# Weight sums by accumulating transfers, parts of 4, 6, 6 and 6, and square sums behind the chain in a two-layer decoder trunk

## The chip, the cores and the metric

The kernel runs on one core of one Trainium2 chip. The metric is the device time of one execution in microseconds (us). It was timed in three runs before the change: median 2678.73 us, from 2677.65 to 2682.8. The times inside an execution come from one profiled execution. Engines are named as the profile names them: PE (matmul), PEld (its weight load), DVE (vector), ACT (scalar), POOL (GpSimd), SP (sync). SP issues most transfers, POOL the others; L12 is line 12 of the kernel before.

## The reference

Two layers, each with an FFN, a mixer (retention and a short gated convolution in parallel) and a second FFN, all with RMS norms before and after, over 512 prompt tokens and 32 sample tokens. All in float32. What the change touches is the FFN and the norms between the phases:

```
def rmsnorm(x, g):
    xf = x.astype(jnp.float32)
    y = xf * lax.rsqrt(jnp.mean(xf * xf, axis=-1, keepdims=True) + NORM_EPS)
    return (y * g.astype(jnp.float32)).astype(x.dtype)

def swiglu(x, w_up, w_down):
    gate, up = jnp.split(x @ w_up, 2, axis=-1)
    return (jax.nn.silu(gate) * up) @ w_down

def layer(x, pos, s0, buf0, norms, w_ffn1_up, w_ffn1_down, w_in, conv_w, w_ret_out, w_conv_out, w_o,
          w_ffn2_up, w_ffn2_down):
    h = x + 0.5 * rmsnorm(swiglu(rmsnorm(x, norms[0]), w_ffn1_up, w_ffn1_down), norms[1])
    m, s_new, buf_new = mixer(rmsnorm(h, norms[2]), pos, s0, buf0, w_in, conv_w, w_ret_out, w_conv_out, w_o)
    h = h + rmsnorm(m, norms[3])
    h = h + 0.5 * rmsnorm(swiglu(rmsnorm(h, norms[4]), w_ffn2_up, w_ffn2_down), norms[5])
    return h, s_new, buf_new
```

The model width is 1024, the FFN width 2816; the mixer's input projection has 64 tiles of 128 columns.

## The kernel before, in words

Tokens lie on the free axis: 544 in two halves of 272. Features lie on the 128 partitions, so the width of 1024 is 8 tiles. A float32 product is made of three matmuls of a reduced format: both operands are cut into a rounded part and a rest (hi and lo for weights, xh and xl for data), and hi·xh, hi·xl and lo·xh are summed in PSUM. Cutting a weight tile is one ACT copy (whi) and one DVE subtraction (wlo).

There are six phases: FFN, mixer, FFN, then the same for the second layer. A phase is a list of jobs, run in order on PE. A plain `Job` (`run`, L335) makes one output tile of 128 features: 8 steps over the width, two halves, three matmuls, 48 in all. A `Pair` (`run_pair`, L353) makes two such tiles (gate and up, of one FFN tile) by seven products in place of eight, 7 × 12 = 84 matmuls in place of 96. The seven products read four weight sets: A (the first weight tile w1 as it is), and with w1 = [a1 a2] and w2 = [b1 b2] the sums s1 = a1 + b1, s3 = b1 + b2 (set 13), s2 = s3 + a1, s4 = s2 + a2 (set 24), and b2 itself (set 22). On the data side they read sums of x that are built once for a phase by `build_ops` (ops b, oh, ol; L587 to L600 and L264). The products run in the order A, 13, 24, A, 13, 24, 22 (the third one, with set 24, adds into a bank that ACT seeds at L194 from the first product's bank).

`PARTS` (L31) cuts the 22 tiles of the FFN width into four parts. In the first, gate and up are plain jobs (`PLAIN_PARTS`), in the others pairs. Behind a part's gate and up jobs come its 8 down jobs, whose length goes with the part's width: n tiles wide is n × 6 matmuls. So the FFN has 17 pairs (a mixer has 17 as well), 102 in all. `BUILD_AT` (L33) names the jobs of the FFN behind which the four `build_ops` are called.

Weights come by SP from HBM into `raw` tiles (L229), `RAW_BUFS` = 3 of them in turn; cut weights live in `w` tiles, `W_BUFS` = 14. A pair's preparation is a list of steps (`pair_steps`, L267): `s_a` cuts A; `s_13` adds s1 and s3 on DVE (L278, L279), `s_24` adds s2 and s4 on DVE (L284, L285) and frees w1's raw tile, which issues the next load; `c_24`, `c_13` and `c_22` cut the sets, the last frees w2's raw tile. `run_pair` calls one step behind each product, for the pair that follows, and `run` calls up to two steps of pairs up to `LOOK` = 4 jobs ahead. From such program order the tile framework makes each engine's queue and its semaphores; code under `urgent` (the seed L194, the evacuations) is moved ahead in it.

At the five boundaries between phases (`boundary`) the order on DVE, ACT and POOL is written out by hand as a script of events with times. The last `TAIL` = 5 down jobs of the old phase and the first `HEAD` = 5 jobs of the new one are run half by half, so that the norm of one half lies beside the matmuls of the other. For each half `chain` makes, for each of 8 tiles, a scaling (L1165), an add to the residual x (L1169), xh on ACT and xl (L1150), and the square (ACT L442) that DVE adds into acc (L444, the last one L448). Then `rstd` sums acc over features on PE (L469, a matmul with ones), and ACT L481 and DVE L482 to L484 make r, the factor of the norm, by which the evacuations multiply (L512, L520). `SUMS` holds the times of the square sums in the script, `RSTD_HEAD` that of the sum over features, `later_prep` cuts weights at given times.

Of the kernel before, what the change touches and what calls it, by code (L numbers as in the profile page):

```python
# [9 lines left out]
F32 = mybir.dt.float32  # L10
F32R = mybir.dt.float32r
AF = mybir.ActivationFunctionType  # L12
ALU = mybir.AluOpType
# [14 lines left out]
P = 128  # L28
KT = DM // P
FT = DFF // P  # L30
PARTS = [(0, 5), (5, 10), (10, 15), (15, 22)]  # L31
PLAIN_PARTS = 1
BUILD_AT = (6, 9, 11, 13)  # L33
CONV_PLAIN = 2
BUILD_MIX = (0, 2, 4, 5)
EPS = 1e-6
# [8 lines left out]

I_Q, I_K, I_V, I_G, I_BG, I_CG, I_XC, I_GR, I_GC = 0, 4, 8, 16, 24, 32, 40, 48, 56

RAW_BUFS = 3
W_BUFS = 14
LOOK = 4  # L50
U_BUFS = 54
T_BUFS = 14
# [7 lines left out]
LAST_B = 1.2  # L60
ONES_B = 4.2
CHAIN_B = 5.0
SUMS = 11.0, 19.0
URGENT = 300
RSTD_HEAD = 17.5, 22.5


def log_gammas():
# [63 lines left out]
class Trunk:  # L132
# [76 lines left out]
    def plan(self):  # L209

        for i, j in enumerate(self.jobs):
            if isinstance(j, Pair):
                a, b = self.to_load(j.w1), self.to_load(j.w2)
                self.steps += [(i, fn) for fn in self.pair_steps(i, a, b)]
            else:
                self.load_of[i] = a = self.to_load(j.w)
                self.steps.append((i, lambda i=i, a=a: self.prep_hi(i, a)(self.nc.vector)))
            self.last_step[i] = len(self.steps)
# [5 lines left out]
    def load(self, upto):  # L224
        while self.n_loaded < min(upto, len(self.loads)):
            w = self.loads[self.n_loaded]
            n = w.shape[1]
            r = self.wp.tile([P, 1024], F32, tag="raw", bufs=RAW_BUFS, name=self.name("raw"))
            self.nc.sync.dma_start(out=r[:, :n], in_=w)  # L229
            self.raw[self.n_loaded] = (r, n)  # L230
            self.n_loaded += 1

# [31 lines left out]
        self.nc.vector.tensor_tensor(out=lo, in0=r, in1=hi.bitcast(F32), op=ALU.subtract)  # L264
        return hl

    def pair_steps(self, i, a, b):  # L267
        nc, d = self.nc, {}
        hl = self.hl[i] = {}
        H = slice(0, 512), slice(512, 1024)  # L270

        def s_a():
            hl["A"] = self.cut(self.parts_of_weights(), self.loaded(a)[0])

        def s_13():
            ra, rb = self.loaded(a)[0], self.loaded(b)[0]
            s = d["13"] = self.w("s13", F32)
            nc.vector.tensor_tensor(out=s[:, H[0]], in0=ra[:, H[0]], in1=rb[:, H[0]], op=ALU.add)  # L278
            nc.vector.tensor_tensor(out=s[:, H[1]], in0=rb[:, H[0]], in1=rb[:, H[1]], op=ALU.add)  # L279

        def s_24():
            ra, s1 = self.raw[a][0], d["13"][:, H[1]]
            s = d["24"] = self.w("s24", F32)
            nc.vector.tensor_tensor(out=s[:, H[0]], in0=s1, in1=ra[:, H[0]], op=ALU.add)  # L284
            nc.vector.tensor_tensor(out=s[:, H[1]], in0=s[:, H[0]], in1=ra[:, H[1]], op=ALU.add)  # L285
            self.freed(a)

        def c_24():
            hl["24"] = self.cut(self.parts_of_weights(), d.pop("24"))

        def c_13():
            hl["13"] = self.cut(self.parts_of_weights(), d.pop("13"))

        def c_22():
            v = self.w("v")
            hl["22"] = self.cut((v[:, H[0]], v[:, H[1]]), self.raw[b][0][:, H[1]])
            self.freed(b)

        return [s_a, s_13, s_24, c_24, c_13, c_22]

    def step_on(self, n, upto=10 ** 6):
        while n > 0 and self.n_stepped < len(self.steps) and self.steps[self.n_stepped][0] < upto:
# [192 lines left out]
    def ffn_jobs(self, ph):  # L495
# [4 lines left out]
        ph["y"] = {}  # L500
        for pi, (p0, p1) in enumerate(PARTS):
            hh = {}
# [51 lines left out]
            def dn(m, pi=pi, p0=p0, p1=p1, hh=hh):  # L554
                last = pi == len(PARTS) - 1

# [600 lines left out]
    def chain(self, ev, at, ph, nxt, half):  # L1157

        nc, s = self.nc, self.hs(half)
        ts = {}  # L1160
        step = STEP if nxt else 0.8

        def scale(f):
            t = ts[f] = self.t("yg")
            nc.vector.tensor_tensor(out=t, in0=ph["y"][f][:, s], in1=ph["ry"][:, s], op=ALU.mult)  # L1165

        def add(f):
            x = self.x[f][:, s]
            nc.vector.tensor_tensor(out=x, in0=x, in1=ts.pop(f), op=ALU.add)  # L1169
            if nxt is None:  # L1170
                nc.sync.dma_start(out=self.a["y"][f, :, s], in_=x)

        for f in range(KT):
            t = at + step * f
            ev(t, lambda f=f: scale(f))
            ev(t + step + 0.4, lambda f=f: add(f))
            if nxt is not None:
                ev(t + step + 0.8, lambda f=f: self.pre_hi(nxt, f, half))
                ev(t + 2 * step + 0.8, lambda f=f: self.pre_lo(nxt, f, half))
                ev(SUMS[half] + 0.45 * f, lambda f=f: self.pre_sum(nxt, f, half, None, nc.vector))  # L1180

    def finish(self, ev, ph, d):

# [52 lines left out]
    def boundary(self, ph, nxt, i):  # L1236
# [3 lines left out]
        nc, script = self.nc, []  # L1240
# [7 lines left out]
        d = len(mvs[0]) * 3 * MM  # L1248
# [27 lines left out]
        if nxt is None:  # L1276
            self.finish(ev, ph, d)
        else:
            ev(LAST_B, lambda: ph["last"].pop()())
            ev(ONES_B, lambda: self.rstd([ph["yacc"][:, self.hs(1)]], 1, ph["ry"], DM))  # L1280
            self.chain(ev, CHAIN_B, ph, nxt, 1)
            V, G = nc.vector, nc.gpsimd
            self.head_script(ev, nxt, i + TAIL)
            for hi, lo in ((tb + d + 0.3, tb + d + 1.3), (tb + 2 * d + 0.3, tb + 2 * d + 1.3), (1.0, 2.0), (6.0, 7.0),
                           (14.0, 15.0)):
                self.later_prep(ev, hi, lo, V)
        self.play(script)
        if nxt is not None:
# [24 lines left out]
    def head_script(self, ev, nxt, i0):  # L1313

        nc = self.nc
        d = KT * 3 * MM
        if nxt["kind"] == "mix":
            self.mix_start(nxt)
        banks, out = [], []

        def copy(n, half):
            if half == 0:
                out.append(self.u("out"))
            nc.scalar.activation(out=out[n][:, self.hs(half)], in_=banks[half][n][:, :HALF], func=AF.Copy)  # L1324
            self.give(banks[half][n])

        for half in range(2):
            banks.append(self.head_part(ev, half * HEAD * d, nxt, i0, half))
            for n in range(HEAD):
                ev((HEAD * half + max(3, n + 1)) * d + 0.1 + 0.3 * n * (n < 3), lambda n=n, half=half: copy(n, half))  # L1330

        def rest(half):
            todo = []
            first = (3, 4) if nxt["kind"] == "mix" else ()
            for n in (*first, *(n for n in range(HEAD) if n not in first)):
                if n == 0 and first:
                    self.mix_tables(nxt, half)
                todo.append(self.jobs[i0 + n].evac(half, out[n][:, self.hs(half)]))
            for fn in todo:
                if fn:  # L1340
                    fn()

        for half in range(2):
            ev(RSTD_HEAD[half], lambda half=half: self.rstd([nxt["acc"][:, self.hs(half)]], half, nxt["r"], DM))
        ev(RSTD_HEAD[1] + 0.1, lambda: rest(0))
        nxt["rest"] = rest

    def head_side(self, nxt):
# [199 lines left out]
```

## Time and profile before

| what | value |
| --- | --- |
| median of three runs | 2678.73 us (2677.65 to 2682.8) |
| the profiled execution's own time | 2677.17 us |
| its span, first to last instruction | 2675.3 us |
| granted clock of PE | 0.997 of full speed |
| PE busy | 2628.3 us, 98%, 20718 matmuls recorded |
| DVE, ACT, POOL busy | 1861.0 (70%), 1354.0 (51%), 237.3 us (9%) |
| bytes moved by DMA | 296.86 MB, 111 GB/s over the span |

The profile counts the time of an engine in instructions as busy; matmuls are pipelined, so a busy PE need not be at its peak. The trace gives, for each instruction, when it started and what ended the idle time before it.

### The profile page before, as it was taken

Reading aid. Unit: us, or ns where it says so; the run is one execution under the profiler, and the core shown is the slowest. Engines: PE = TensorE matmul, PEld = TensorE weight load, DVE = VectorE, ACT = ScalarE, POOL = GpSimd, SP = SyncE. Lnnn points to the kernel's source line nnn. Section 1 sums busy time; section 2 is a strip of 40 time slices with the busy share of each in tenths; the row PEclk is TensorE's granted clock in tenths of the full one; section 3 lists DMA queues with packets and bytes.
Section 4 is the critical chain, followed back from the end, with each engine's and each line's share of the span. In section 5 each row is a group of like instructions: output and inputs, shape, how many; then the busy total and the mean of one; then the engine's idle time right before and its main releaser. Section 6 shows DMA issues by size and latency. Waiting matters only on the chain. (4 is left out here: it accounts for less than half of the span.)

```text
span 2675.3 us, 50606 instructions
## 1 busy us (share of the span) xinstructions
PE 2628.3 (98%) x20718; PEld 2606.1 (97%) x20718; DVE 1861.0 (70%) x3213; ACT 1354.0 (51%) x2546; POOL 237.3 (9%) x375
## 2 busy tenths in 40 slices
PE   9999999999999999999999999999999999999998
PEld 9999998999999999999999999999999999999997
DVE  6756748677986487667488557587678764875673
ACT  6555554434553455555555555544345434655553
POOL 1000021222100100000100000211210001000002
PEclk9999999999999999999999999999999999999999
DMA  4233344333343432332432334343333433323332
GB/s 155 83 96 102 105 142 148 116 107 120 103 132 104 133 106 83 99 103 86 130 118 84 101 95 144 114 147 105 111 116 101 130 104 121 118 83 95 102 105 90
DMA packets 91977, 296.86 MB, mean 111 GB/s; under 512 B 12064, under 2 KB 16288, under 8 KB 91744
## 3 DMA queue, kind: packets, MB, share of 16 engines
q1 hardware_dynamic: 74592, 235.46, 28.9%
q0 software_dynamic: 17152, 58.16, 6.3%
q8 instruction: 162, 2.65, 0.4%
q14 instruction: 71, 0.58, 0.1%
HBM read 266.17 MB, written 27.41 MB: 110 GB/s over the span
## 5 line engine op out<-in xcount | busy, mean ns | idle before, releaser
L324 PE MATMUL banks<-oh,whi 128*128 128x272 f32 x2040 | 588.6, 289 | 3.0 <-ACT banks L194 1.6
L324 PE MATMUL banks<-oh,wlo 128*128 128x272 f32 x2040 | 587.9, 288 | 0.0
L324 PE MATMUL banks<-ol,whi 128*128 128x272 f32 x2040 | 586.6, 288 | 0.0
L324 PE MATMUL banks<-xh,whi 128*128 128x272 f32 x1600 | 455.2, 298 | 9.6 <-ACT out L1324 8.7
L324 PE MATMUL banks<-xl,whi 128*128 128x272 f32 x1600 | 442.4, 289 | 0.0
L252 ACT ACTIVATE whi<-raw 128x1024 fp32r<-128x1024 f32 (+2 forms) x273 | 253.5, 931 | 313.3 <-PE banks L324 248.4
L256 DVE TENSOR_TENSOR wlo<-raw,whi 128x1024 fp32r<-128x1024 f32 (+2 forms) x273 | 291.2, 1068 | 150.5 <-ACT whi L252 117.6
L324 PEld LDWEIGHTS banks<-oh,whi 128*128 128x128 f32 x2040 | 383.8, 188 | 6.4 <-ACT banks L194 2.8
L324 PE MATMUL banks<-hh,whi 128*128 128x272 f32 x1408 | 385.2, 289 | 0.1
L324 PE MATMUL banks<-hl,whi 128*128 128x272 f32 x1408 | 384.5, 288 | 0.2
L324 PEld LDWEIGHTS banks<-ol,whi 128*128 128x128 f32 x2040 | 384.5, 188 | 0.0
L324 PEld LDWEIGHTS banks<-oh,wlo 128*128 128x128 f32 x2040 | 383.9, 188 | 0.0
L324 PE MATMUL banks<-xh,wlo 128*128 128x272 f32 x1600 | 371.5, 289 | 0.4 <-DVE wlo L1395 0.4
L264 DVE TENSOR_TENSOR wlo<-s,whi 128x1024 fp32r<-128x1024 f32 x204 | 249.7, 1224 | 102.8 <-ACT whi L263 50.5
L324 PEld LDWEIGHTS banks<-xh,whi 128*128 128x128 f32 x1600 | 303.4, 190 | 13.2 <-ACT out L1324 10.0
L324 PE MATMUL banks<-hh,wlo 128*128 128x272 f32 x1408 | 313.3, 288 | 0.0
L324 PEld LDWEIGHTS banks<-xl,whi 128*128 128x128 f32 x1600 | 303.4, 190 | 2.1 <-DVE xl L1150 1.0
L263 ACT ACTIVATE whi<-s 128x1024 fp32r<-128x1024 f32 x204 | 214.8, 1055 | 141.3 <-PE banks L324 97.8
L324 PEld LDWEIGHTS banks<-xh,wlo 128*128 128x128 f32 x1600 | 267.9, 190 | 1.1 <-DVE wlo L1395 1.1
L324 PEld LDWEIGHTS banks<-hh,whi 128*128 128x128 f32 x1408 | 264.9, 188 | 0.9 <-ACT banks L194 0.8
L324 PEld LDWEIGHTS banks<-hl,whi 128*128 128x128 f32 x1408 | 264.8, 188 | 0.8 <-DVE hl L547 0.6
L324 PEld LDWEIGHTS banks<-hh,wlo 128*128 128x128 f32 x1408 | 229.6, 188 | 0.0
(246 smaller groups left out, 4993.3 us busy)
## 6 DMA issues: line engine op xcount, KB each, us to landing
raw<-in_w_up SPq DMA_DIRECT2D x173, 512.0 KB, 3.6
raw<-in_w_in SPq DMA_DIRECT2D x128, 512.0 KB, 3.6
raw<-in_w_down SPq DMA_DIRECT2D x96, 320.0 KB, 3.0
raw<-in_w_down SPq DMA_DIRECT2D x32, 448.0 KB, 4.0
xd<-x POOLq DMA_DIRECT2D x40, 272.0 KB, 2.7
x<-xd POOLq DMA_DIRECT2D x40, 272.0 KB, 4.9
s<-in_state_ret POOLq DMA_DIRECT2D x32, 256.0 KB, 3.5
out_ret_s<-s POOLq DMA_DIRECT2D x32, 256.0 KB, 2.9
```

Of the source, the lines that this page charges most:

```text
L252: self.nc.scalar.activation(out=hi[:, :n], in_=r[:, :n], func=AF.Copy)
L256: eng.tensor_tensor(out=lo[:, :n], in0=r[:, :n], in1=hi[:, :n].bitcast(F32), op=ALU.subtract)
L263: self.nc.scalar.activation(out=hi, in_=r, func=AF.Copy)
L264: self.nc.vector.tensor_tensor(out=lo, in0=r, in1=hi.bitcast(F32), op=ALU.subtract)
L324: self.nc.tensor.matmul(out=ps[:, :HALF], lhsT=w, rhs=x, start=start, stop=stop, skip_group_check=again)
```

## The change

In each pair, s1 and s3 are no longer added on DVE. A staging tile takes [a1 b1] by two transfers of SP, 256 KB each, and then a transfer of POOL adds the whole of w2 = [b1 b2] onto it, which leaves [s1 s3]. From w2 itself only b2 is loaded beside it (256 KB in place of 512). The step `s_13` is gone, `s_24` reads s3 from the staging tile and `c_13` cuts that tile. One more raw tile and one fewer w tile are held. The parts are 4, 6, 6 and 6 tiles wide, so an FFN has 18 pairs, and all phases together 106; the `build_ops` come one to four jobs earlier. At the boundaries the square sums, their `rstd`, the rest of half 0 and one weight cut have other places in the script.

```
-PARTS = [(0, 5), (5, 10), (10, 15), (15, 22)]
+PARTS = [(0, 4), (4, 10), (10, 16), (16, 22)]
-BUILD_AT = (6, 9, 11, 13)
+BUILD_AT = (5, 6, 8, 9)
-RAW_BUFS = 3
-W_BUFS = 14
+RAW_BUFS = 4
+W_BUFS = 13
-SUMS = 11.0, 19.0
+SUMS = 17.6, 18.2
-RSTD_HEAD = 17.5, 22.5
+RSTD_HEAD = 18.3, 22.1
...
-                a, b = self.to_load(j.w1), self.to_load(j.w2)
-                self.steps += [(i, fn) for fn in self.pair_steps(i, a, b)]
+                a, s, b = self.to_load(j.w1), self.to_load((j.w1, j.w2)), self.to_load(j.w2[:, 512:])
+                self.steps += [(i, fn) for fn in self.pair_steps(i, a, s, b)]
...
-            n = w.shape[1]
-            self.nc.sync.dma_start(out=r[:, :n], in_=w)
+            if isinstance(w, tuple):
+                n = 1024
+                for k, x in enumerate(w):
+                    self.nc.sync.dma_start(out=r[:, 512 * k:512 * k + 512], in_=x[:, :512])
+                self.nc.gpsimd.dma_start(out=r, in_=w[1], accum_op=ALU.add)
+            else:
+                n = w.shape[1]
+                self.nc.sync.dma_start(out=r[:, :n], in_=w)
...
-        def s_13():
-            ra, rb = self.loaded(a)[0], self.loaded(b)[0]
-            s = d["13"] = self.w("s13", F32)
-            nc.vector.tensor_tensor(out=s[:, H[0]], in0=ra[:, H[0]], in1=rb[:, H[0]], op=ALU.add)
-            nc.vector.tensor_tensor(out=s[:, H[1]], in0=rb[:, H[0]], in1=rb[:, H[1]], op=ALU.add)
-
         def s_24():
-            ra, s1 = self.raw[a][0], d["13"][:, H[1]]
+            ra, s1 = self.raw[a][0], self.loaded(s13)[0][:, H[1]]
...
         def c_13():
-            hl["13"] = self.cut(self.parts_of_weights(), d.pop("13"))
+            hl["13"] = self.cut(self.parts_of_weights(), self.raw[s13][0])
+            self.freed(s13)
 
         def c_22():
             v = self.w("v")
-            hl["22"] = self.cut((v[:, H[0]], v[:, H[1]]), self.raw[b][0][:, H[1]])
+            hl["22"] = self.cut((v[:, H[0]], v[:, H[1]]), self.loaded(b)[0][:, H[0]])
             self.freed(b)
 
-        return [s_a, s_13, s_24, c_24, c_13, c_22]
+        return [s_a, s_24, c_24, c_13, c_22]
...
-                ev(SUMS[half] + 0.45 * f, lambda f=f: self.pre_sum(nxt, f, half, None, nc.vector))
+                ev(SUMS[half] + 0.05 * f, lambda f=f: self.pre_sum(nxt, f, half, None, nc.vector))
...
             for hi, lo in ((tb + d + 0.3, tb + d + 1.3), (tb + 2 * d + 0.3, tb + 2 * d + 1.3), (1.0, 2.0), (6.0, 7.0),
-                           (14.0, 15.0)):
+                           (18.7, 18.8)):
...
-        ev(RSTD_HEAD[1] + 0.1, lambda: rest(0))
+        ev(RSTD_HEAD[1] + 0.05, lambda: rest(0))
```

The first place is DVE's queue in the first FFN, over one pair of the steady stretch. L278 and L279 are `s_13`, L284 and L285 `s_24`, L264 the cuts, L400 and L408 PSUM evacuations, L542 and L547 what follows them. Before:

```order
L408 TENSOR_TENSOR c_242_1379<-banks,p_241_1378 128x272
L278 TENSOR_TENSOR s_259_1510<-raw_1273,raw_1364 128x512
L279 TENSOR_TENSOR s_259_1510<-raw_1364 128x512
L542 SCALAR_TENSOR_TENSOR g_1410<-c_242_1379,g_1410 128x272
L284 TENSOR_TENSOR s_262_1527<-s_259_1510,raw_1273 128x512
L542 SCALAR_TENSOR_TENSOR g_1410<-banks,g_1410 128x272
L285 TENSOR_TENSOR s_262_1527<-s_262_1527,raw_1273 128x512
L547 TENSOR_TENSOR hl_1462<-g_1410,hh_1461 128x544
L264 TENSOR_TENSOR wlo_1546<-s_262_1527,whi_1545 128x1024
```

With the change (line numbers are two to six higher there; `raw_1345` is a staging tile, `raw_1237` w1):

```order
L410 TENSOR_TENSOR c_243_1327<-banks,p_242_1326 128x272
L270 TENSOR_TENSOR wlo_1436<-raw_1237,whi_1435 128x1024
L285 TENSOR_TENSOR s_263_1467<-raw_1345,raw_1237 128x512
L544 SCALAR_TENSOR_TENSOR g_1361<-c_243_1327,g_1361 128x272
L286 TENSOR_TENSOR s_263_1467<-s_263_1467,raw_1237 128x512
L544 SCALAR_TENSOR_TENSOR g_1361<-banks,g_1361 128x272
L270 TENSOR_TENSOR wlo_1489<-s_263_1467,whi_1488 128x1024
L549 TENSOR_TENSOR hl_1419<-g_1361,hh_1418 128x544
L270 TENSOR_TENSOR wlo_1506<-raw_1345,whi_1505 128x1024
```

Two adds are gone, the first add of `s_24` reads the staging tile, and the second product's cut (the last row) reads it too.

The second place is POOL's queue, which issues the accumulating transfers. With the change, in the first FFN:

```order
L232 DMA raw_171_916<-in_w_up 128x1024
L232 DMA raw_201_1045<-in_w_up 128x1024
L232 DMA raw_221_1152<-in_w_up 128x1024
L232 DMA raw_245_1345<-in_w_up 128x1024
L232 DMA raw_264_1470<-in_w_up 128x1024
L232 DMA raw_283_1595<-in_w_up 128x1024
```

Before there is no such row; they stand one behind another, each behind the two loads of SP that fill its tile.

The third place is DVE's queue at the boundary from the third phase to the fourth, for the first half: L1165, L1169 and L1150 are the chain, L444 and L448 the square sums. Before:

```order
L444 TENSOR_TENSOR acc_15346<-acc_15346,sq_15854 128x272
L1165 TENSOR_TENSOR yg_15857<-y_12320,ry_15345 128x272
L444 TENSOR_TENSOR acc_15346<-acc_15346,sq_15859 128x272
L1169 TENSOR_TENSOR x_15320<-x_15320,yg_15822 128x272
L1150 SCALAR_TENSOR_TENSOR xl_15359<-x_15319,par,xh_15351 128x272
L444 TENSOR_TENSOR acc_15346<-acc_15346,sq_15865 128x272
L444 TENSOR_TENSOR acc_15346<-acc_15346,sq_15868 128x272
L1165 TENSOR_TENSOR yg_15871<-y_12362,ry_15345 128x272
```

With the change (the same chain, L1152 in place of L1150, L446 and L450 the sums):

```order
L1152 SCALAR_TENSOR_TENSOR xl_15443<-x_15403,par,xh_15435 128x272
L1152 SCALAR_TENSOR_TENSOR xl_15444<-x_15404,par,xh_15436 128x272
L446 TENSOR_TENSOR acc_15427<-acc_15427,sq_15962 128x272
L446 TENSOR_TENSOR acc_15427<-acc_15427,sq_15965 128x272
L446 TENSOR_TENSOR acc_15427<-acc_15427,sq_15968 128x272
L446 TENSOR_TENSOR acc_15427<-acc_15427,sq_15971 128x272
L446 TENSOR_TENSOR acc_15427<-acc_15427,sq_15974 128x272
L446 TENSOR_TENSOR acc_15427<-acc_15427,sq_15977 128x272
L450 SCALAR_TENSOR_TENSOR acc_15427<-sq_15980,acc_15427 128x272
```

The seven adds, which lay between the rows of the chain, now stand in one run behind its last row. PE's sum over features of the first half stands 9 matmuls later than before, that of the second half 28 matmuls behind it in place of 61.

The fourth place is DVE's queue behind the last plain job of that FFN, whose result (L522, L526, L528; L520, L524, L526 before) is the last that the down jobs wait for; `ol` are operands of the pairs, from `build_ops`. With the change:

```order
L522 TENSOR_TENSOR tu_16411<-banks,r_15428 128x272
L270 TENSOR_TENSOR ol_16348<-t_2556_16334,oh_16347 128x544
L526 TENSOR_TENSOR tu_16411<-tu_16411,sg_16322 128x272
L270 TENSOR_TENSOR ol_16352<-t_2557_16335,oh_16351 128x544
L528 TENSOR_TENSOR hl_16410<-tu_16411,hh_16409 128x272
L522 TENSOR_TENSOR tu_16416<-banks,r_15428 128x272
L262 TENSOR_TENSOR wlo_16482<-raw_16179,whi_16481 128x512
L526 TENSOR_TENSOR tu_16416<-tu_16416,sg_16325 128x272
L528 TENSOR_TENSOR hl_16410<-tu_16416,hh_16409 128x272
```

Before, the same evacuation stands together, with one weight cut inside it:

```order
L520 TENSOR_TENSOR tu_16459<-banks,r_15347 128x272
L520 TENSOR_TENSOR tu_16464<-banks,r_15347 128x272
L524 TENSOR_TENSOR tu_16459<-tu_16459,sg_16397 128x272
L524 TENSOR_TENSOR tu_16464<-tu_16464,sg_16400 128x272
L256 TENSOR_TENSOR wlo_16602<-raw_16407,whi_16601 128x640
L526 TENSOR_TENSOR hl_16458<-tu_16459,hh_16457 128x272
L526 TENSOR_TENSOR hl_16458<-tu_16464,hh_16457 128x272
```

Operands of the pairs are now built between the rows of that evacuation.

## Rows read from the trace of the kernel before

**Rows 1.** The page: the span, and busy time, share and instructions of each engine.

```profile
span 2675.3 us, 50606 instructions
PE 2628.3 (98%) x20718; PEld 2606.1 (97%) x20718; DVE 1861.0 (70%) x3213; ACT 1354.0 (51%) x2546; POOL 237.3 (9%) x375
```

**Rows 2.** Busy time of each engine in one stretch of the first FFN (clock, DMA share, GB/s last).

```profile
150.00:200.00 50.00, 50.00 (x402) 50.00 (x402) 26.14 (x36) 24.86 (x52) 0.00 (x0) 1.00 0.29 88
```

**Rows 3.** ACT's seeds L194 from 195 to 225 us: durations, first and last start.

```profile
L194 ACT ACTIVATE banks<-banks x3: 378/380/380, 200.2 to 221.2; 128x272 f32<-128x272 f32 x3
```

**Rows 4.** What PE waited for, longest first: us in total, times, longest us.

```profile
PE banks L469 <- DVE acc L448: 15.4, 10, 1.6
PE banks L324 <- ACT out L1324: 8.7, 6, 2.8
```

**Rows 5.** PE's timeline at the third boundary (start, us, instruction, idle before it).

```profile
1353.72 0.29 PE L324 MATMUL banks<-xh,wlo 128*128 128x272 f32 x1
1355.47 0.72 PE L469 MATMUL banks<-acc,ones 128*128 128x272 f32 x2 [1.46 <-DVE acc L448]
...
1363.68 0.29 PE L324 MATMUL banks<-xh,wlo 128*128 128x272 f32 x1
1365.56 0.73 PE L469 MATMUL banks<-acc,ones 128*128 128x272 f32 x2 [1.59 <-DVE acc L448]
...
1375.72 0.39 PE L324 MATMUL banks<-xh,whi 128*128 128x272 f32 x1 [0.40 <-ACT out L1324]
```

**Rows 6.** DVE's timeline at the third boundary: square sums among the chain, then r.

```profile
1348.42 0.45 DVE L444 TENSOR_TENSOR acc<-acc,sq 128x272 f32<-128x272 f32 x1 [0.78 <-ACT sq L442]
...
1350.83 0.99 DVE L444 TENSOR_TENSOR acc<-acc,sq 128x272 f32<-128x272 f32 x2 [0.50 <-ACT sq L442]
...
1354.98 0.44 DVE L448 SCALAR_TENSOR_TENSOR acc<-sq,acc 128x272 f32<-128x272 f32 x1 [0.75 <-ACT sq L442]
...
1356.10 1.22 DVE L256 TENSOR_TENSOR wlo<-raw,whi 128x1024 fp32r<-128x1024 f32 x1
...
1359.13 0.50 DVE L1150 SCALAR_TENSOR_TENSOR xl<-x,par,xh 128x272 fp32r<-128x272 f32 x1
...
1361.94 2.08 DVE L444 TENSOR_TENSOR acc<-acc,sq 128x272 f32<-128x272 f32 x4
```

**Rows 7.** DVE by line and shape over the execution: busy us, mean ns, idle before.

```profile
L278 DVE TENSOR_TENSOR s<-raw,raw 128x512 f32<-128x512 f32 x102 | 69.9, 685 | 23.5 <-DMA raw<-in_w_in 12.0 <-PE banks L324 11.5
L279 DVE TENSOR_TENSOR s<-raw 128x512 f32<-128x512 f32 x102 | 69.8, 685 | 0.0
```

**Rows 8.** The page: DMA issues, KB each, median us from issue to landing.

```profile
raw<-in_w_up SPq DMA_DIRECT2D x173, 512.0 KB, 3.6
...
x<-xd POOLq DMA_DIRECT2D x40, 272.0 KB, 4.9
s<-in_state_ret POOLq DMA_DIRECT2D x32, 256.0 KB, 3.5
```

**Rows 9.** DVE's timeline over one pair of the first FFN, from the first add on.

```profile
208.09 0.69 DVE L284 TENSOR_TENSOR s<-s,raw 128x512 f32<-128x512 f32 x1
208.69 0.43 DVE L542 SCALAR_TENSOR_TENSOR g<-banks,g 128x272 f32<-128x272 f32 x1
209.04 0.68 DVE L285 TENSOR_TENSOR s<-s,raw 128x512 f32<-128x512 f32 x1
209.85 0.72 DVE L547 TENSOR_TENSOR hl<-g,hh 128x544 fp32r<-128x544 f32 x1
210.86 2.56 DVE L264 TENSOR_TENSOR wlo<-s,whi 128x1024 fp32r<-128x1024 f32 x2 [0.28 <-ACT whi L263]
```

**Rows 10.** SP's timeline over the same pair: the load that L285 sets free.

```profile
209.79 0.33 SPq L229 DMA_DIRECT2D raw<-in_w_up  x1
```

**Rows 11.** DVE's timeline in the third FFN, from r to the first pairs' sums.

```profile
1369.67 0.44 DVE L484 SCALAR_TENSOR_TENSOR r<-yq,y 128x272 f32<-128x272 f32 x1
...
1399.90 0.79 DVE L520 TENSOR_TENSOR tu<-banks,r 128x272 f32<-128x272 f32 x2 [4.46 <-PE banks L324]
...
1402.04 0.79 DVE L526 TENSOR_TENSOR hl<-tu,hh 128x272 fp32r<-128x272 f32 x2
1402.74 1.48 DVE L587 SCALAR_TENSOR_TENSOR n<-x,par,r 128x544 f32<-128x544 f32 x2
...
1428.83 0.69 DVE L285 TENSOR_TENSOR s<-s,raw 128x512 f32<-128x512 f32 x1
```

**Rows 12.** PE's timeline in the third FFN: where it first reads the last hl.

```profile
1402.83 0.29 PE L324 MATMUL banks<-hh,whi 128*128 128x272 f32 x1
1402.96 0.29 PE L324 MATMUL banks<-hl,whi 128*128 128x272 f32 x1
```

More of the change, by code (lines that the diff above doesn't have):

```diff
@@ L265, in cut, with pair_steps @@
         return hl
-    def pair_steps(self, i, a, b):
+    def pair_steps(self, i, a, s13, b):
         nc, d = self.nc, {}
```

## Prediction, made before the changed kernel was run

> **What bounds the kernel now.** I read the page first: PE is busy for 2628.3 of 2675.3 us, DVE 70%, ACT 51% [rows 1]. So time goes only where PE has fewer matmuls or waits less. A stretch in the middle of an FFN says how fast PE then is: in 50 us it issues 402 matmuls without a gap, 0.1244 us each [rows 2]; three seeds of three pairs lie 200.2 to 221.2 us, a pair is 10.5 us, 84 matmuls at 0.125 [rows 3]. Next come PE's waits. Two groups hold nearly everything between phases: L469, the sum of squares over features, waited 10 times for the last square add, 15.4 us, and L324 waited 6 times for ACT's copies L1324, 8.7 us [rows 4]. That is 24.1 us at five boundaries, 4.8 us each, and nothing of this size stands inside an FFN.
>
> The sum is made on the profiled execution, 2677.17 us, of which 1.9 us lie outside its span; the median of the runs is 1.6 us higher. A measurement of this kernel tells 0.2%, about 5.4 us, from no change.
>
> **Parts 4, 6, 6, 6.** One more FFN tile of each FFN goes from two plain jobs (96 matmuls) to a pair (84). Four FFNs × 12 = 48 matmuls × 0.125 = **−6.0 us** on PE itself, the one sure term.
>
> **The two adds.** L278 and L279 fall away: 102 × (685 + 685) ns = 139.7 us of DVE [rows 7]. They hide behind PE's matmuls now, so I cost this at 0. It lowers the cover that DVE needs: the seed L194 and the evacuations behind them in the queue come earlier, never later, as long as the staging tile is there in time.
>
> **The staging tile.** This is the price of the adds, a loop from pair to pair. The second add of `s_24` frees w1's raw tile; SP issues the next load 0.07 us later, 209.79 against 209.72 [rows 9, 10], and each issue takes it 0.33 us. The staging tile of the next pair takes that slot: two issues (0.66), the landing of the second, then POOL's accumulating transfer A, and only then may the next pair's first add start. For a load of 256 KB I take 3.5 us, as the state load, and 512 KB takes 3.6 [rows 8]. So from freed to summed: 0.07 + 0.33 + 3.5 + A = 3.9 + A. First to second add with the evacuation between them is 208.09 to 209.72, 1.63 us [rows 9]. The loop fits in 10.5 us as long as A is at most 4.9. No accumulating transfer is in this trace. The nearest rows: 3.6 for 512 KB by SP, and 4.9 for 272 KB by POOL in bursts of eight [rows 8]. Both fit; the other end is that every byte costs twice, 7.2. I take 4.2, between the near rows, and the loop costs 0. What is queued behind the waiting first add on DVE is the gate's evacuation, the second add, then `hl` and two weight cuts [rows 9]; ACT's cut of set 24 and, right behind it, the seed L194 for PE's third product wait with them. So if the loop is too long, PE stops at that product, in every pair. On POOL's own queue the transfers stand in a row behind one another in an FFN, and nothing else is late there, POOL being 9% busy [rows 1]; in the mixers they stand among copies and spills.
>
> The Trainium skill speaks against this step: "Collectives: The Full Stack", in the part on the bandwidth ceiling, says that a transfer that adds needs two source reads on the same ring and runs at about half the rate of a copy. By that A would be nearer 7.2 than 3.6, and the time that of the second rival below; no run here shows it yet.
>
> **The boundaries.** Take the third one. PE stands from 1353.72 to 1355.47 for half 0, from 1363.68 to 1365.56 for half 1, and 0.4 us for the copies [rows 5]. The seven square adds of half 0 lie among the chain, and DVE idles before three of them for squares from ACT, 0.78 + 0.50 + 0.75 us [rows 6]. With the change the chain runs through and the adds stand behind it. The chain's last row ended at 1359.63; without the adds (7 × 0.35), their idle time (2.0) and the two weight cuts that lay among the last rows (2 × 1.14), it ends at 1352.9. Then seven dependent adds, 0.545 us apart (2.08 us for four [rows 6]), end near 1356.6. PE reaches its sum 9 matmuls later than before, 1353.85 + 1.1 = 1354.95: a wait of about 1.6 in place of 1.6 to 1.75. For half 1 the adds end near 1361.7, behind r of half 0, and PE's sum, 28 matmuls behind the first, is due at 1360.8: a wait of 1.0 in place of 1.9. The third wait goes, as r comes before the copies are wanted. That is about 1.7 us here; boundaries into a mixer, whose third waits are up to 2.8 [rows 4], give a little more. I take 1.8 × 5 = **−9.0 us**. The ends: 0, if the waits only change place, and −24.1, all of them gone.
>
> **The first part of an FFN.** It loses a tile: two plain jobs (96 matmuls) and 8 × 6 matmuls of down jobs, 144 × 0.125 = 18 us of cover less, for the same four builds of the pairs' operands. Before, DVE idled 4.46 us ahead of the last plain job's evacuation at 1399.90, and its result `hl` was there at 1402.83, when PE was about to read it at 1402.96 [rows 11, 12]: 0.13 us of slack. With the change I counted DVE's queue from r to the last `hl`: 43 rows of 272 columns at 0.352, 6 of 544 at 0.635, 4 at 0.70 and 5 weight cuts at 0.60 make 24.8 us, with no idle. PE is there 22.8 us after r's start (the rest of its head, three plain jobs, 21 matmuls). So PE may stand **2.0 us** at its first down job. Then the first `s_24` ends some 37.9 us after r; the second pair's staging tile takes its slot and is summed 3.9 + A = 8.1 later, two adds, one cut, two evacuations, one more cut and the seed make 4.9, so the seed ends at 50.9; PE wants it at 47.1. Counted so, a wait of 3.8 us for each FFN, the 2.0 within it. This is an upper end, as the queue is counted back to back and r is taken at its latest; the lower end is 0. Before, the second pair's last add ended at 1429.51 (1428.83 + 0.69) and PE lost nothing [rows 11]. I take a little over the middle, 2.2 × 4 = **+9 us**.
>
> **The sum.** −6.0 − 9.0 + 9 = −6.0: **2671 us**, a small gain, with a range of its own from 2664 to 2675.
>
> **The rivals.**
> 1. *The first parts cost their full price.* For it: the count above, and that the cover was down to 0.13 us. Against: four builds moved earlier, and DVE was idle there before. Time: 2677.2 − 6 − 9 + 4 × 3.8 = 2677, with A at its upper near row 2680. Chance 0.20, mostly no change.
> 2. *The accumulating transfer is slow* (the other side). Point of decision: A = 4.9 us. Each 0.1 us above makes every pair in a chain longer by that; in a group of six FFN pairs some three links count (two are prepared under down jobs, the last has no follower), in a mixer's longest stretch six: 12 × 3 + 2 × 6 = 48 links. A = 5.5 gives 48 × 0.6 = +29, 2700; A = 6 gives +53, 2724; A = 7.2 gives +110, 2781. For it: the added traffic, 1.75 MB for each pair in place of 1.0, and the adding itself. Against: the load on the DMA engines in an FFN is 0.29 [rows 2]. Chance 0.22, some 0.12 of it for bytes that cost twice (A from 5.5 up).
> 3. *The boundaries give more*: the half-1 sums come in time as well. 3 us more at each: 2671 − 15 = 2656. Chance 0.10.
> 4. *The boundary part does nothing*: the sums wait behind the chain as long as before, only elsewhere. Then 2677.2 − 6 − 0 + 9 = 2680, with less in the first parts 2675. Chance 0.06, no change.
>
> **How the numbers follow.** Forecast 0.42 (0.40 faster, 0.02 same), rival 1 0.20 (0.13 same, 0.07 slower), rival 2 0.22 (slower), rival 3 0.10 (faster), rival 4 0.06 (0.05 same, 0.01 slower). Faster 0.50, same 0.20, slower 0.30. The range goes down to 2655 (rival 3) and up to 2710, which takes rival 2 to A = 5.7; what lies above, about half of that rival, and a little below 2655 is left out.
>
> **What would show it.** A pair's period in the middle of an FFN (seeds 10.5 us apart) and no PE wait on L194: the loop fits; a longer period with DVE waiting for the staging tile is rival 2, and the accumulating transfer's landing time says by how much. PE's waits at L471 (L469 before): 15.4 should fall to about 13, and those for L1326 from 8.7 to near nothing. A PE wait on `hl` at the first down job of each FFN, or on the seed of the first or second pair, prices the first parts: 9 us in all is my term, 0 or 15 its ends. Wrong would be a time above 2683 or below 2660.

## The result, and the profile after

The changed kernel took **2871.93 us** (median of four runs, 2866.93 to 2872.64), the kernel before 2679.07 beside it: a ratio of 1.0714, 95% interval 1.0695 to 1.0732. It is 193 us slower, where 6 us less was forecast, and lies far above the range.

The page of the changed kernel, as [rows 1], and its transfers, as [rows 8]:

```profile
span 2870.1 us, 51404 instructions
...
PE 2687.1 (94%) x20670; PEld 2649.8 (92%) x20670; DVE 1748.6 (61%) x3013; ACT 1352.8 (47%) x2558; POOL 331.4 (12%) x481
...
raw<-in_w_up SPq DMA_DIRECT2D x222, 256.0 KB, 3.0
...
raw<-in_w_up POOLq DMA_DIRECT2D x72, 512.0 KB, 6.2
...
raw<-in_w_in POOLq DMA_DIRECT2D x34, 512.0 KB, 6.2
```

The 48 matmuls are gone (20718 to 20670), and so are 112 us of DVE. Yet PE is busy for 59 us more, and idle for 183 us of the span (6%) where it was 47: the 136 us more of idle time and the 59 of busy time are the whole 195 by which the span grew. The adding transfer lands 6.2 us after its issue; 4.2 were taken and 4.9 was the limit. What PE waits for, as [rows 4] (line numbers are two higher):

```profile
PE banks L326 <- ACT banks L194: 109.4, 58, 5.1
PE banks L326 <- ACT out L1326: 14.8, 6, 3.3
PE banks L471 <- DVE acc L450: 10.8, 10, 1.2
PE banks L326 <- ACT hh L527: 7.8, 8, 1.4
```

The first line was 1.6 us before and is now 58 waits for the seed, 109.4 us, most of the added idle time. The waits on the square sums fell (15.4 to 10.8), those on the copies rose (8.7 to 14.8), and one for `hh` came in. Now one turn of the loop, in DVE's timeline of the first FFN, where [rows 9] showed no idle time:

```profile
225.55 0.69 DVE L285 TENSOR_TENSOR s<-raw,raw 128x512 f32<-128x512 f32 x1 [3.00 <-DMA raw<-in_w_up]
...
226.51 0.68 DVE L286 TENSOR_TENSOR s<-s,raw 128x512 f32<-128x512 f32 x1
...
237.62 0.69 DVE L285 TENSOR_TENSOR s<-raw,raw 128x512 f32<-128x512 f32 x1 [0.55 <-DMA raw<-in_w_up]
...
249.87 0.69 DVE L285 TENSOR_TENSOR s<-raw,raw 128x512 f32<-128x512 f32 x1 [2.19 <-DMA raw<-in_w_up]
```

SP's and POOL's timelines between the first two of these sums:

```profile
227.26 0.81 SPq L231 DMA_DIRECT2D raw<-in_w_up  x2
```

```profile
231.18 0.86 POOL L232 DMA_DIRECT2D raw<-in_w_up  x1 [11.81 <-ACT p L399]
```

The second add ends at 227.19 and frees w1's tile; SP issues the two loads at 227.26; POOL issues the adding transfer at 231.18, when they have landed; the next pair's first add starts at 237.62. That is 3.99 us for the loads, as reckoned (3.9), and 6.44 for the adding transfer. The sums of the pairs lie 12.07 and 12.25 us apart, where PE's matmuls take 10.5. PE, in the same pair:

```profile
226.65 0.28 PE L326 MATMUL banks<-oh,wlo 128*128 128x272 f32 x1
229.17 0.39 PE L326 MATMUL banks<-oh,whi 128*128 128x272 f32 x1 [2.23 <-ACT banks L194]
...
231.03 0.43 PE L326 MATMUL banks<-oh,whi 128*128 128x272 f32 x1
231.26 0.43 PE L326 MATMUL banks<-ol,whi 128*128 128x272 f32 x1
```

It stands ahead of the third product, the one that the seed L194 opens, as the second rival said. The last two rows come behind the stall: the matmuls there start 0.23 us apart, where they start 0.125 apart elsewhere.

It isn't only the pairs that follow one another. In the mixer, where a plain job stands between two pairs, five seeds lie 21.2 us apart (84.7 / 4); the seeds of the same five pairs lay 17.1 apart before (68.3 / 4). First after, then before:

```profile
L194 ACT ACTIVATE banks<-banks x5: 378/379/380, 858.1 to 942.8; 128x272 f32<-128x272 f32 x5
```

```profile
L194 ACT ACTIVATE banks<-banks x5: 379/381/383, 806.8 to 875.1; 128x272 f32<-128x272 f32 x5
```

The loop is another one there. The plain job's own load stands in the row of tiles, so the next staging tile takes the slot of the staging tile before it, which is free only when `c_13` has cut that tile. That is some 10 us later in a pair than the sums of `s_24`. DVE's timeline, and SP's behind the cut:

```profile
877.27 0.69 DVE L285 TENSOR_TENSOR s<-raw,raw 128x512 f32<-128x512 f32 x1 [7.67 <-DMA raw<-in_w_in]
...
887.32 1.23 DVE L270 TENSOR_TENSOR wlo<-raw,whi 128x1024 fp32r<-128x1024 f32 x1
...
898.70 0.69 DVE L285 TENSOR_TENSOR s<-raw,raw 128x512 f32<-128x512 f32 x1 [6.30 <-DMA raw<-in_w_in]
```

```profile
888.57 0.80 SPq L231 DMA_DIRECT2D raw<-in_w_in  x2
```

The cut ends at 888.55, SP issues the loads at 888.57, and the next first add starts 21.4 us behind the one before.

PE's granted clock falls in these stretches too. PE of the changed kernel in three stretches (clock, DMA share and GB/s last), then the kernel before in one of them:

```profile
700.00:750.00 50.00, 43.79 (x317) 42.59 (x318) 38.52 (x63) 26.08 (x45) 6.96 (x15) 0.93 0.58 151
850.00:900.00 50.00, 44.30 (x317) 43.52 (x315) 20.39 (x31) 13.06 (x22) 3.85 (x6) 0.90 0.49 127
900.00:950.00 50.00, 43.66 (x305) 43.07 (x306) 22.97 (x35) 16.63 (x28) 2.29 (x3) 0.90 0.42 111
```

```profile
850.00:900.00 50.00, 49.91 (x393) 49.29 (x393) 30.44 (x45) 20.01 (x33) 0.54 (x1) 1.00 0.38 121
```

A mean of 0.90 means that PE ran a part of the stretch at 1.2 GHz and the rest at 2.4; it came with the stalls, one for each pair there. Over the span the clock is 0.977, before 0.997. That is where the 59 us of PE's added busy time are from: 43.66 us busy would hold 351 matmuls at 0.1244 us, and 305 ran.

### The profile page after: what moved, and what is told of

Same layout as the page of the kernel before. It is cut to its first block, busy times and chain, and to the rows that moved or that the text cites. A ratio compares the mean times of both kernels' runs of the same rounds, so it can differ in the third digit from the quotient of the medians.

```text
span 2870.1 us, 51404 instructions
## 1 busy us (share of the span) xinstructions
PE 2687.1 (94%) x20670; PEld 2649.8 (92%) x20670; DVE 1748.6 (61%) x3013; ACT 1352.8 (47%) x2558; POOL 331.4 (12%) x481
## 5 line engine op out<-in xcount | busy, mean ns | idle before, releaser
L326 PE MATMUL banks<-oh,whi 128*128 128x272 f32 x2120 | 638.0, 301 | 117.5 <-ACT banks L194 109.4
L326 PE MATMUL banks<-oh,wlo 128*128 128x272 f32 x2120 | 628.7, 297 | 0.0
L326 PE MATMUL banks<-ol,whi 128*128 128x272 f32 x2120 | 628.6, 297 | 0.0
L326 PEld LDWEIGHTS banks<-oh,whi 128*128 128x128 f32 x2120 | 418.1, 197 | 134.1 <-ACT banks L194 122.8
L326 PE MATMUL banks<-xh,whi 128*128 128x272 f32 x1472 | 420.1, 298 | 16.9 <-ACT out L1326 14.8
L326 PEld LDWEIGHTS banks<-ol,whi 128*128 128x128 f32 x2120 | 418.7, 197 | 0.0
L326 PE MATMUL banks<-xl,whi 128*128 128x272 f32 x1472 | 407.2, 289 | 2.4 <-DVE xl L1152 2.4
L270 DVE TENSOR_TENSOR wlo<-raw,whi 128x1024 fp32r<-128x1024 f32 x212 | 259.1, 1222 | 85.4 <-PE banks L326 48.3
L269 ACT ACTIVATE whi<-s 128x1024 fp32r<-128x1024 f32 x106 | 112.2, 1059 | 324.1 <-DVE s L286 297.8
L269 ACT ACTIVATE whi<-raw 128x1024 fp32r<-128x1024 f32 x212 | 222.7, 1050 | 86.5 <-PE banks L326 83.7
```

The source lines that it names most:

```text
L269: self.nc.scalar.activation(out=hi, in_=r, func=AF.Copy)
L326: self.nc.tensor.matmul(out=ps[:, :HALF], lhsT=w, rhs=x, start=start, stop=stop, skip_group_check=again)
```

## The experiments

Three theories were set against each other. The loop theory: the staging tile's turn (a slot freed late, two loads, the adding transfer) is longer than a pair. Rival C: the added 83 MB of traffic slow every load. Rival P: the loss sits in the shorter first part and the boundaries. Medians are in us; each ratio is to the kernel before, run beside it.

| run | median | ratio, 95% interval |
| --- | --- | --- |
| the change | 2871.93 | 1.0714 (1.0695 to 1.0732) |
| e1, sums by DVE | 2693.39 | 1.0053 (1.0041 to 1.0066) |
| e2, staging alone | 2818.2 | 1.0514 (1.0495 to 1.0534) |
| e4, plain transfer | 2731.42 | 1.0211 (1.0192 to 1.0230) |
| e5, staging first | 2736.08 | 1.0218 (1.0204 to 1.0232) |
| e13, staging first, plain | 2695.34 | 1.0065 (1.0051 to 1.0078) |
| e8, staging first, alone | 2721.16 | 1.0160 (1.0144 to 1.0176) |
| e6, boundary alone | 2691.33 | 1.0043 (1.0030 to 1.0055) |
| e7, parts alone | 2690.26 | 1.0040 (1.0027 to 1.0052) |
| e9, boundary, rest at +0.3 | 2666.35 | 0.9949 (0.9937 to 0.9962) |
| e10, e9 and parts, builds 5, 8, 9, 10 | 2694.23 | 1.0057 (1.0044 to 1.0070) |
| e11, as e10 with parts 4, 5, 6, 7 | 2690.85 | 1.0046 (1.0033 to 1.0059) |
| e14, 13 w tiles alone | 2674.01 | 0.9985 (0.9976 to 0.9994) |
| e15, e9 with 13 w tiles | 2664.49 | 0.9949 (0.9936 to 0.9961) |
| e16, e10 with builds 5, 7, 9, 11 | 2682.64 | 1.0019 (1.0010 to 1.0028) |
| e17, e11 with builds 5, 7, 9, 11 | 2684.41 | 1.0021 (1.0011 to 1.0030) |

**Which part holds the loss.** e1 takes the staging tile out of the change, e2 puts it alone into the kernel before.

```
# e1, against the change: load, plan and pair_steps as before
+RAW_BUFS = 3
+W_BUFS = 14
# e2, against the kernel before: load, plan and pair_steps of the change
+RAW_BUFS = 4
+W_BUFS = 13
```

> The change with the two weight sums added on DVE again (three raw tiles, fourteen w tiles, w2 loaded whole), parts, builds and boundaries as in the change. Loop theory (the loss is the loop from a freed raw tile over two loads and the accumulating transfer to the next pair's first add, 10.4 + 1.6 us against a pair's 10.5): the whole loss goes, 2660 to 2685 us. Rival P (the loss sits in the shorter first part and the boundaries): it stays above 2800. Rival C (the added 83 MB of traffic slow all loads): as the loop theory, the traffic being gone.

> The kernel before with nothing but the staging tile (and its 4 raw and 13 w tiles): old parts, builds and boundaries. Loop theory and rival C: the loss is all here, 2855 to 2890 us, slightly less for 102 pairs in place of 106. Rival P: near 2679.

e1 came out at 2693.39, e2 at 2818.2. So the staging tile carries 178 of the 193 us (2871.93 − 2693.39), and rival P is out as the main cause; but e1 lies 15 us above before, more than the loop theory had allowed, and e2 stays 37 us under its expectation. The rest of the change (parts and boundaries) and the staging tile make each other worse by 2871.93 − 2693.39 − (2818.2 − 2678.63) = 39 us. In e2 PE waited 80.1 us for the seed and 26.3 for the square sums, in e1 0.8 for the seed.

**Loop, traffic or adding.** e4 leaves the adding out: the transfer of POOL is a plain one. e5 keeps all transfers, loads the staging tile first of a pair's three and cuts it before the sums of set 24, so that, where pair follows pair, it takes the slot which the last but one pair frees with its last cut. e13 is e5 with the plain transfer. (In e4 and e13 the staging tile holds w2 itself and not the sums.)

```
# e4
-                self.nc.gpsimd.dma_start(out=r, in_=w[1], accum_op=ALU.add)
+                self.nc.gpsimd.dma_start(out=r, in_=w[1])
# e5
-                a, s, b = self.to_load(j.w1), self.to_load((j.w1, j.w2)), self.to_load(j.w2[:, 512:])
+                s, a, b = self.to_load((j.w1, j.w2)), self.to_load(j.w1), self.to_load(j.w2[:, 512:])
...
+            self.freed(s13)
             self.freed(a)
...
-        return [s_a, s_24, c_24, c_13, c_22]
+        return [s_a, c_13, s_24, c_24, c_22]
```

> The change with the accumulating transfer of POOL made a plain one of the same size from the same place: nothing is added, so the sums are wrong, the bytes written, the queue and the waits are the same. Loop theory: landing falls from 6.2 to about 4.5 us, the loop to 8.4 + 1.6, below 10.5; the waits on the seed mostly go, 2670 to 2720 us. Rival C (traffic): the bytes are the same but for the second read, it stays above 2800.

> The change with the staging tile loaded first of a pair's three tiles (order s, a, b) and cut before the sums of set 24, so that its slot is the one that the last pair but one frees with its last cut, not the one that the sums of the pair before free: some 8 us more for the same transfers. Loop theory: the wait goes, a pair is 10.5 us again, 2660 to 2710 us. Rival C: the same bytes and the same adding transfers, it stays above 2800.

> The changed kernel with the staging tile loaded first (2736.08 us) and POOL's transfer plain, so nothing is added and the sums are wrong. What is left there over the run with DVE adds is 43 us. If the adding itself is the rest (landing 5.6 and 7.2 against 4.2 and 4.5 us): 2695 to 2710. If it is the bytes and the queues (rival C): 2725 to 2740.

e4 took 2731.42, e5 2736.08: each alone takes some 140 us away, 11 and 26 us above what the loop theory had said, and some 65 under what rival C had. PE's waits for the seed in e5, then the same and the transfers of POOL in e4:

```profile
PE banks L326 <- ACT banks L194: 21.9, 31, 2.5
```

```profile
PE banks L326 <- ACT banks L194: 24.6, 16, 3.2
...
raw<-in_w_up POOLq DMA_DIRECT2D x72, 512.0 KB, 4.2
...
raw<-in_w_in POOLq DMA_DIRECT2D x34, 512.0 KB, 4.5
```

DVE's first add (L285) waited for transfers for 207.8 us in the change, for 84.0 in e4 and not at all in e5, where the bytes, the queue and the adding are the same as in the change (ACT's cut of the staging tile now comes first, and takes the wait over). The loop is thus shown twice: by shortening it and by starting it earlier. In the first FFN the sums of e4 lie 10.5 us apart again:

```profile
219.41 0.69 DVE L285 TENSOR_TENSOR s<-raw,raw 128x512 f32<-128x512 f32 x1
...
229.89 0.69 DVE L285 TENSOR_TENSOR s<-raw,raw 128x512 f32<-128x512 f32 x1
```

What e4 leaves is largely the mixers' other loop: 63.7 of its 84.0 us are there, and the five seeds lie 18.1 us apart; in e13 it is 16.4. e13, with both changes, took 2695.34, 2 us above e1. Leaving DVE's adds out can't have hidden much of a cost, as with them PE waited for the seed only 0.8 us (e1). So the traffic itself costs next to nothing, and rival C is out; the 41 us between e5 and e13 are the adding. Its queue shows it, as queue, packets, MB and share of 16 engines; the change first, then e13:

```profile
q0 software_dynamic: 32416, 113.74, 17.4%
```

```profile
q0 software_dynamic: 32416, 113.74, 12.5%
```

The bytes are equal. In engine time it is 0.174 × 2870.1 = 499 us against 0.125 × 2691.6 = 336. POOL's queue before the change had 58.16 MB at 6.3%, 169 us. If that part of the queue is unchanged, the 55.6 MB of the staging transfers took 331 us adding and 168 us plain, a factor of 1.97.

e8 is e5's order alone in the kernel before.

> The kernel before with the staging tile alone, loaded first of a pair's three. Loop theory: what is left of the 140 us of staging alone is some part of the 43 that the same order leaves in the changed kernel, 2690 to 2725 us. Rival C (traffic): above 2760.

2721.16, inside the loop theory's range: staging costs 41 us in the old parts too, even when it starts early. PE waited 23.1 us for the seed and 26.4 for the square sums at the old boundaries. It isn't worth the adds it saves in any form that was tried, since those lay beside PE's work.

**The boundary.** e6 is the boundary's part of the change alone, e9 the same but for one time.

```
# e6, against the kernel before
-SUMS = 11.0, 19.0
+SUMS = 17.6, 18.2
-RSTD_HEAD = 17.5, 22.5
+RSTD_HEAD = 18.3, 22.1
-                ev(SUMS[half] + 0.45 * f, ...)
+                ev(SUMS[half] + 0.05 * f, ...)
-                           (14.0, 15.0)):
+                           (18.7, 18.8)):
-        ev(RSTD_HEAD[1] + 0.1, lambda: rest(0))
+        ev(RSTD_HEAD[1] + 0.05, lambda: rest(0))
# e9, against e6
-        ev(RSTD_HEAD[1] + 0.05, lambda: rest(0))
+        ev(RSTD_HEAD[1] + 0.3, lambda: rest(0))
```

> The kernel before with the change's boundary alone (times of the square sums, of their sum over features, of the rest of half 0 and of one weight cut). In the run with DVE adds, PE's waits on the square sums fell from 15.4 to 10.7 us, those on the copies of half 1 rose from 8.7 to 12.8. Theory A (the copy that stood ahead of ACT's table load and sigmoids now stands behind them, since the rest of half 0 comes at 22.15 and the copy at 22.3): about nothing gained, 2674 to 2683 us, the waits on copies at 11 or more. Rival, as forecast (the boundary gains 9, the loss is in the parts alone): 2666 to 2672.

> The boundary alone, with the rest of half 0 at +0.3 in place of +0.05, so that ACT's first copy of half 1 stands ahead of the table load and the sigmoids again. Theory A: the waits on copies fall to 8 us or less with those on square sums at 11, 2668 to 2675 us. Rival (the copies are late for another reason): as the boundary alone.

e6 took 2691.33, 11 us slower than before and 8 above its range; e9 2666.35, 25 us less and better than expected. The first copy of half 1 has the time (5 + 3) × 24 × 0.1157 + 0.1 = 22.3 in the script. Before, the rest of half 0 (ACT's table load, sigmoids and hh) came at 22.6, behind it; in the change at 22.15, ahead of it. ACT's timeline at the third boundary, e6 and then e9:

```profile
1373.08 1.28 ACT L513 ACT_TABLE_LOAD   x1
...
1378.40 1.52 ACT L1324 ACTIVATE out<-banks 128x272 f32<-128x272 f32 x5
```

```profile
1358.00 0.39 ACT L1324 ACTIVATE out<-banks 128x272 f32<-128x272 f32 x1
...
1363.23 1.28 ACT L513 ACT_TABLE_LOAD   x1
...
1368.88 1.24 ACT L1324 ACTIVATE out<-banks 128x272 f32<-128x272 f32 x4
```

With all five copies behind the table load, no bank is free for the next job, and PE stands; e6 at that place, and then e9's waits in all:

```profile
1378.83 0.59 PE L324 MATMUL banks<-xh,whi 128*128 128x272 f32 x1 [5.22 <-ACT out L1324]
```

```profile
PE banks L469 <- DVE acc L448: 12.2, 10, 1.6
...
PE banks L324 <- ACT out L1324: 1.7, 2, 1.0
```

In e6 the copies cost 20.1 us, in e9 1.7, before 8.7.

**The parts.** e7 is parts and build places alone. e10, e11, e16 and e17 stand on e9, with other parts and build places.

```
# e7, against the kernel before (e10 and e16: the same parts on e9)
-PARTS = [(0, 5), (5, 10), (10, 15), (15, 22)]
+PARTS = [(0, 4), (4, 10), (10, 16), (16, 22)]
-BUILD_AT = (6, 9, 11, 13)
+BUILD_AT = (5, 6, 8, 9)
# e10 and e11: BUILD_AT = (5, 8, 9, 10); e16 and e17: (5, 7, 9, 11)
# e11 and e17: PARTS = [(0, 4), (4, 9), (9, 15), (15, 22)]
```

> The kernel before with the parts 4, 6, 6, 6 and their build places alone. Theory A (the shorter first part costs a wait at the first down job of each FFN, some 2.5 us with the slower clock behind it, and 48 matmuls are saved): 2677 to 2688 us, with the wait on hh at the first down jobs. Rival (the parts save their 6 us, the boundary spoils them): 2668 to 2674.

> The boundary with the rest at +0.3 (2666.35 us), DVE adds, and the parts 4, 6, 6, 6 with the builds behind jobs 5, 8, 9, 10 in place of 5, 6, 8, 9, so that no build stands in DVE's queue behind the last two plain jobs. Theory A (the parts alone cost 10 because a build is mixed into the last plain job's evacuation): the wait at the first down job goes and the 6 us of matmuls stay, 2659 to 2667 us. Rival (the shorter first part leaves DVE no room at all): the wait moves to the first pair's seed, 2672 to 2690.

> As the run with builds behind 5, 8, 9, 10, but parts 4, 5, 6, 7, so that the last part keeps its 7 tiles and the boundary its old length. Theory A: the same 18 pairs without the wait on xl at the boundary (2.5 us in the parts alone), 2656 to 2665 us. Rival: no better than parts 4, 6, 6, 6.

> The boundary with the rest at +0.3, parts 4, 6, 6, 6, builds behind jobs 5, 7, 9, 11, some 6 us apart from the second on, where one takes DVE 5.1. If the builds only stood too close: the waits on y and hh go, 2658 to 2667 us. If the first part has too little room: the wait moves to the first pair's b or seed, 2672 to 2692.

> The same with parts 4, 5, 6, 7, which keep the boundary's length. If the builds stood too close: 2656 to 2665 us. If there is too little room: as with parts 4, 6, 6, 6, less some 2.5.

e7 took 2690.26, 10 us above before and 2 above its range, so the parts cost 16 if they save the 6 that 48 matmuls take. PE's timeline of e7 in the third FFN, at its first down job:

```profile
1014.61 0.39 PE L324 MATMUL banks<-hh,whi 128*128 128x272 f32 x1 [1.14 <-ACT hh L525]
1016.06 0.39 PE L324 MATMUL banks<-hl,whi 128*128 128x272 f32 x1 [1.06 <-DVE hl L526]
1016.88 0.39 PE L324 MATMUL banks<-hh,whi 128*128 128x272 f32 x1 [0.42 <-ACT hh L525]
```

That is the wait for which the count of DVE's queue had given 2.0 us, and 2.6 at this FFN; in all, 7.3 us for hh, 4.2 for hl, and 2.5 for xl at the boundaries, whose last down jobs are shorter. PE's busy time also rose by 1.7 us (2630.0 against 2628.3) with 48 matmuls fewer, so some 8 us of the 16 are matmuls that ran slower; the granted clock is 0.995. Builds placed later didn't save it. In e10 the wait is gone from there and stands in a later down job, one of 4.9 us for each FFN, for ACT's copy y, which lies in ACT's queue behind the builds' `oh` and weight cuts that wait for DVE:

```profile
1417.26 0.59 PE L324 MATMUL banks<-hh,whi 128*128 128x272 f32 x1 [4.87 <-ACT y L566]
```

Both theories missed its place: not hh, not the seed, but y. Spaced wider, e16 waits 3.3 us there, 12.9 in all against 19.4, and is 12 us faster than e10; e17 is no better than e16. So the builds do stand too close, but no spacing that was tried brought the wait under the 6 us that the parts save, and e16 is still 16 us above e9. Whether another order of DVE's queue would is open.

**One w tile fewer.** The staging tile's slot is paid with a w tile.

```
# e14, against the kernel before; e15, against e9
-W_BUFS = 14
+W_BUFS = 13
```

> The kernel before with 13 w tiles in place of 14, nothing else. With the staging tile at the old boundaries, PE's waits on the square sums were 26.4 us, 15.4 before. If the missing w tile does that (a weight cut waits for PE in front of the last adds): waits of 24 to 28 us and 2688 to 2698 us. Rival (the transfers do it): 2676 to 2683.

> The boundary with the rest at +0.3 (2666.35 us) and 13 w tiles in place of 14. If the fewer tiles help by the copies' wait alone (8.7 to 3.1 us in the kernel before, square sums 15.4 to 21.3), which the boundary has removed already: no gain, 2664 to 2676 us. If they help apart from the boundary: 2659 to 2664.

e14 took 2674.01, a little faster than before and below both ranges. The waits on square sums rose from 15.4 to 21.3, the way the first branch said but short of its 24, and those on the copies fell from 8.7 to 3.1. So the 26.4 of e8 are not the missing tile's alone. With the boundary of e9 it gives 2664.49, the lowest median here, 14 us under before; the ratio is that of e9.

## Why the prediction was wrong, by its own steps

- *What bounds the kernel* was right: PE, its waits at the boundaries, none inside an FFN. The change made new ones.
- *The two adds cost 0*: right in kind. DVE lost 112 us of work and nothing came of it. No run leaves the adds out without the staging tile, but with them PE waited for the seed only 1.6 us (0.8 in e1), so there was little to gain.
- **The staging tile is the step that failed**: "I take 4.2, and the loop costs 0". Where pair follows pair, the loop was described as it runs, its loads were right (3.99 against 3.9), and the point of decision, 4.9 us, too. The adding transfer took 6.2 to its landing, outside the rows that I held to be near. A plain transfer of the same size from the same queue takes 4.2 (e4): the rows gave the plain price, and the adding was left out. The second rival, at 0.22, is what happened.
- *Its price* was too low as well: the second rival went up to 2781 at A = 7.2, and 2872 was measured at 6.2. At A = 6.2 its 48 links give 48 × 1.3 = 62 us; the waits on the seed are 109.4, in 58 places. In the turn shown the transfer took 6.44 from POOL's issue to the add, so a pair takes 12.07 us and the next one 12.25, 1.6 to 1.75 above 10.5. The mixers' pairs with a plain job between them were left out of the links; there the slot is freed by `c_13` and not by the sums, and they run 21.2 us apart in place of 17.1. On top comes the slower clock behind the stalls, 59 us more of PE's busy time, which no term had.
- *The Trainium skill*, "Collectives: The Full Stack", the part on the bandwidth ceiling, says of a collective's step that adds that it needs two source reads and runs at about half the rate of one that copies. The trace agrees with the rate: 1.97 times the engine time (331 against 168 us) for the same bytes. That two reads are the reason is shown by no run here. The landing grew by less, from 4.2 to 6.2 us. I gave bytes that cost twice a chance of 0.12.
- *The boundaries, −9*: right for the square sums (15.4 to 10.8, 13 forecast), wrong for the third wait, which "goes" in the prediction and rose from 8.7 to 14.8 us. The boundary as changed costs 11 us by itself (e6). I followed DVE's queue and PE's and not ACT's, where the moved rest stands ahead of the copies. With that one event placed later, the boundary gave 14 us (e9), more than the term.
- *The first parts, +9*: the full count, 15.2 us, is near the 16 of e7, but partly by luck. Of its 3.8 for each FFN it put 2.0 at the first down job, where e7 shows 2.9, and 1.8 at the seed, whose waits rose only from 1.6 to 2.3 us in all. The waits at the shorter boundaries (2.5) and the slower matmuls (some 8) weren't in it. Taking a little over the middle of 0 and the count was a choice without a row behind it.
- *Parts, −6 us of matmuls*: 48 fewer are recorded, and the saving is smaller than what the first part loses.

## What to carry to other kernels

When work is moved from an engine that is not the bound into a transfer, draw the buffer's loop first: what frees the slot, every transfer until it is read, and the period it must fit in; if the loop is longer than the period, every turn pays. Draw it for each order of jobs, as a job in between can move the tile to a slot that is freed later. Price an operation that the trace does not show by what it adds to the nearest row, not by the row itself, and hold a choice between far ends that has no row for a risk. When an event moves in a hand-written order, read every engine's queue at that place: here 0.25 in a script's time, on an engine that looked idle, was worth 25 us.

## What the runs showed that I had not expected

- The adding transfer of 512 KB from HBM onto SBUF lands after 6.2 us, a plain one of the same queue after 4.2; POOL's own issue of it took 0.86 us in the trace (0.87 in the mixers), that of a plain one 0.53 (e4).
- A stall in each pair took the granted clock to a mean of 0.90 over 50 us. Over the span it is 0.977 in the change and 0.997 before, and PE is busy 59 us longer for 48 matmuls fewer, so the stalls cost more than their length. Idle time alone doesn't give the clock: e4 and e5 leave PE idle for 88.6 and 87.3 us, at 0.993 and 0.990, with 16 and 31 waits for the seed.
- One weight tile fewer was no loss: 2674.01 against 2678.72 us (e14).
